# First loads, the order of hi and lo passes, and the issue of weight sums in a two-layer decoder trunk

## The chip, the cores and the metric

One Trainium2 chip, one core in use. The metric is the device time of one launch in microseconds (us). The time of the kernel before is the median of 3 runs; which of two kernels is the faster is judged from such runs.

## The reference

A two-layer trunk on x (256 tokens by 1024) with a memory of 256 rows by 1024, all in fp32. Cut to what matters here:

```python
# layer 0: short gated convolution; layer 1: block-sparse causal attention (one block of 256 here)
b_gate, c_gate, u = jnp.split(h @ w_in, 3, axis=-1)
x = x + (b_gate * causal_conv(c_gate * u)) @ w_out
# both layers: attention to the memory, 4 heads of 256
k, v = jnp.split(rms_norm(mem, g) @ w_kv, 2, axis=-1)
q = rms_norm(x, g) @ w_q
x = x + softmax(q k^T / 16) v @ w_o
# both layers: feed-forward, inner width 2816
g, u = jnp.split(rms_norm(x, g) @ w_gu, 2, axis=-1)
x = x + (silu(g) * u) @ w_down
# after layer 0 one shared k, v is projected from x for layer 1; a last rms_norm ends it
```

The weights are streamed from DRAM.

## The kernel before, in words

**Three passes for one product.** TensorE (PE) works on fp32 data in a rounded form (fp32r). To keep fp32 accuracy each operand is held as hi + lo: ScalarE (ACT) rounds a copy (hi), VectorE (DVE) subtracts it from the original (lo), and PE adds three products in PSUM: hi by hi and hi by lo with the weight's hi part, and lo by hi with the weight's lo part. The tables `(0, 0), (0, 1), (1, 0)` in the code are these passes, weight part first. A weight chunk's lo part is so needed by one pass of three.

**The weight stream.** `weight_plan` (line 69) lists all weight chunks in the order of their use; a chunk is 128x1024 fp32, 512 KB. `Feed` (line 314) moves each through SP's load queue into one of `RAWS` = 5 raw buffers, then through ACT (`split_high`) and DVE (`split_low`) into one of `WBUFS` = 10 pairs of hi and lo, and PE frees the pair. When the lo part of a chunk is made, its raw buffer is free, and the load five chunks on is written to SP's queue. The program is straight-line code for each engine, made at build time: `Clock` (line 184) keeps a rough model of the time of each engine, and `Side` (line 247) uses it to decide where splits, evictions, norms and attention steps go in each engine's order. An engine runs its instructions in that order; a wait at the head of a queue holds all that is behind it. `Feed.hooks` is a table of things to do when the load of a given number is issued.

**The order of the layers.** Keys of the memory for layer 0 (`mem_keys`, line 829, tiles `raw_memk`, `hi_memk`, `lo_memk`, `acc_memk`: eight chunks k, each times eight column groups j); the convolution (`short_conv`, chunks wc, wu, wb, PSUM tiles `cu` and `pb`, four pairs jp of two column groups jj); its output product; memory values and attention; the feed-forward of layer 0; the shared k, q and v of the block attention with keys, output and values of the memory beside them; memory attention; the feed-forward of layer 1; the last norm.

**The start.** `first` (128x568) holds a quarter of the memory, the first 256 columns of key chunk 0 and all gains in one tensor. The rest of chunk 0 comes in two loads (256 and 512 columns), then the second 256-column piece of the memory (`mT_raw`, 128x256), then chunk 1. While these come in, PE runs 13 products on a blank tile (`warm`).

**The feed-forward.** A norm needs a factor `rs` per token, which GpSimd (POOL) computes in one instruction for each of the two token halves h. While the factor of the second half is on its way, PE runs `rows` products (weights wr). `sg` is the silu on ACT, `gg` its product on DVE, `pt_g` the transpose of `gg` on PE. Gate and up weights are wg, wu, the down weights wd.

**Sums of weights.** Gate and up columns are worked on in 11 blocks of 256. For some pairs of blocks, named by their first block in `GROUPS` (8 in layer 0; 4 and 8 in layer 1), the weights of the pair are taken as four quarters B11, B12, B21, B22 and multiplied in a form with seven block products in place of eight (PSUM tile `seven`). It needs four sums, T1 = B11+B12, T3 = B12+B22, T2 = T1+B22, T4 = T2+B21, each in two halves. They are made in DRAM: `sum_steps` (line 532) gives 16 steps for a pair, eight copies on SP's queue (line 550, B to T or T to T) and eight adding transfers on POOL's queue (line 548, `accum_op`). A copy of a sum waits until the adding transfer before it has landed, and an adding transfer waits for its copy. In the kernel before, the steps hang at loads spread evenly: `SUMS_AT` puts layer 0's 16 steps over loads 44 to 104 and layer 1's 32 steps over loads 128 to 220 (lines 1031 to 1034). When their numbers come up, they are issued, whatever is in flight. The sums are read back as weight chunks (`raw_wT`).

**Bank of memory.** The hi and lo parts of the memory are put aside in DRAM and read back for layer 1 by two loads on POOL's queue (`mem_bank`, line 1627, row L1629 of the profile).

All ACT, DVE and POOL work that a helper records has line L242 in the profile, matmuls have L464, transposes L468, loads L481.

Of the kernel before, what the change touches and what calls it, by code (L numbers as in the profile page):

```python
# [42 lines left out]
SPARE = 1500  # L43
LATER = 2000
BANKWISE = 5
GROUPS = ((8,), (4, 8))
SUMS_AT = ((44, 104), (128, 220))

# [20 lines left out]
def weight_plan():  # L69
# [82 lines left out]
    plan = row_plan("memk0", mem_w_kv[0], 0, "memkv0", pieces=2, halves=2)  # L152
    plan[0].update(cuts=(0, T, 2 * T, D), pieces=4)
    for jp in range(4):
# [92 lines left out]
class Side:  # L247
# [3 lines left out]
    def __init__(self, clock, **free):  # L251
        self.clock = clock
        self.open = []
        self.free = {kind: [0.0] * n for kind, n in free.items()}
        self.feed = None

# [20 lines left out]
    def poll(self):  # L277
        for item in sorted(self.open, key=lambda i: i[0]):
            if not item[2] and item[0] <= self.clock.now:
                self.step(item)  # L280
        soon = any(self.clock.now <= i[0] <= self.clock.now + HOLD for i in self.open)
        self.feed.pump(soon)

    def others(self, item=None):
# [91 lines left out]


class Act:

# [19 lines left out]
def yoco_kernel(  # L399
    ctx: ExitStack,  # L400
    tc: tile.TileContext,
    x, mem, positions, norm_ffn, norm_final, xT, memT, first, chunks, conv_wT, out,
):
# [49 lines left out]
    def unit_f32(name, shape):  # L453
        return acts.tile(shape, F32, tag="unit", name=name)
# [32 lines left out]
    def load_chunk(it):  # L487
        raw = raws.tile([P, it["a"], it["b"]], F32, tag="raw", name=f"raw_{it['name']}")
        if "sum" in it:
            load(raw, weight_sums[it["sum"]])  # L490
            return raw
        src = chunks[it["chunk"] * P:(it["chunk"] + 1) * P].rearrange("p (a n) -> p a n", a=it["a"])
        for c in chunk_pieces(it)[1 if "cuts" in it else 0:]:
            load(raw[:, :, c], src[:, :, c], freed=feed.emptied)
        return raw
# [11 lines left out]
    def split_high(it, raw):  # L507
        hi = wts.tile([P, it["a"], it["b"]], F32R, tag="hi", name=f"hi_{it['name']}")
        lo = wts.tile([P, it["a"], it["b"]], F32R, tag="lo", name=f"lo_{it['name']}")
        for c in chunk_pieces(it):  # L510
            if it["gain"] is None:
                scalar.copy(hi[:, :, c], raw[:, :, c])
            elif "cuts" in it:
                scalar.activation(hi[:, 0, c], first_raw if c.start == 0 else raw[:, 0, c], AF.Copy, scale=first_gain)
            else:
                scalar.activation(hi[:, :, c], raw[:, :, c], AF.Copy, scale=gain_col(*it["gain"]))
        return hi, lo

    def split_low(it, raw, hi, lo):
        for c in chunk_pieces(it):  # L520
            if it["gain"] is None:
                vector.tensor_sub(lo[:, :, c], raw[:, :, c], hi[:, :, c])
            elif "cuts" in it:
                vector.scalar_tensor_tensor(lo[:, 0, c], first_raw if c.start == 0 else raw[:, 0, c], first_gain,
                                            hi[:, 0, c], op0=OP.mult, op1=OP.subtract)
# [32 lines left out]

    plan, _, quarters, ffn_steps = weight_plan()
    feed = side.feed = Feed(clock, plan, load_chunk, split_high, split_low)  # L560


# [188 lines left out]
    mT0 = new_act("mT0")  # L751
    first_tile = unit_f32("first", [P, 2 * T + len(GAINS) * KD])
    load(first_tile, first)
    first_mem, first_raw, first_gains = (first_tile[:, c] for c in (slice(0, T), slice(T, 2 * T), slice(2 * T, None)))
    first_gain = first_gains[:, :1]
# [5 lines left out]
    feed.load_to(1)  # L761
    m_turned = [half_tile("mT_raw_0", (P, 2, T))]
    load(m_turned[0][:, 1, :], memT[:P, T:])
    feed.load_to(2)
# [12 lines left out]
    feed.split_next()  # L777
    split(*m_parts[1], m_turned[0][:, 1, :])
    feed.split_next()
    split(*unit_pair(mT0, 1), m_turned[1])  # L780

    def split_rest():
        for i in (2, 3):
# [4 lines left out]
            vector.tensor_sub(lo, m_turned[i], hi)  # L788
        for _ in range(4):
            side.give("half")  # L790
# [38 lines left out]
    def mem_keys(name, mT, wait, scaled=True):  # L829
# [32 lines left out]
        for k in range(KD - 2):  # L862
            w = feed.take(f"{name}_{k}")
            if k == 0:
                for js in ((0, 1), (2, 3), (4, 5, 6, 7)):
                    for one in ((0, 0), (0, 1)):
                        for j in js:
                            step(k, w, j, (one,))
                for j in range(KD):
                    step(k, w, j, ((1, 0),))  # L870
                feed.free()
                continue
# [157 lines left out]
    for l in range(2):  # L1030
        steps = [step for jp in GROUPS[l] for step in sum_steps(l, jp)]
        first, end = SUMS_AT[l]
        for n, step in enumerate(steps):
            feed.hooks.setdefault(first + (end - first) * n // len(steps), []).append(step)


    def short_conv(act, into):
# [34 lines left out]
        for jp in range(4):  # L1072
# [7 lines left out]
            for jj in range(2):  # L1080
# [10 lines left out]
                for i, name in enumerate(("wc", "wu")):  # L1091
# [3 lines left out]
                    jobs.append(side.start(gate_sum(cus[0], pieces[0]) if i == 0 else conv(j, cus[1], pieces, jobs)))  # L1095
                mm_cols(pb, act, wb, jj, 1, last=0)
                mm_cols(pb, act, wb, jj, 0, range(1, KD), last=0)
                if jj:
# [609 lines left out]
def laid_out(inputs):  # L1708
# [16 lines left out]
    return dict(inputs, xT=pairs(inputs["x"][0]), memT=memT, first=first, chunks=chunks.reshape(-1, D),  # L1725
                conv_wT=columns(inputs["conv_w"][0]))


_INS = ["x", "mem", "positions", "norm_ffn", "norm_final", "xT", "memT", "first", "chunks", "conv_wT"]

# [17 lines left out]
```

## Time and profile before

| what | value |
|---|---|
| time, median of 3 runs (lowest to highest) | 786.16 us (785.79 to 787.91) |
| the profiled execution: its own time | 786.73 us |
| its span, first to last instruction | 785.0 us |
| PE busy, matmuls | 773.9 us (99%), 4147 |
| DVE busy | 573.5 us (73%), 872 |
| ACT busy | 459.5 us (59%), 728 |
| POOL busy | 37.7 us (5%), 68 |
| DRAM read and written | 178.82 MB and 28.31 MB |
| mean granted clock of PE | 0.999 |

The span is read on PE: the other engines run beside it. PE is idle for 785.0 - 773.9 = 11.1 us, at a few places, and a change that doesn't alter PE's work moves the time through these places or through new ones. A row of the timeline gives start, length, engine, line, operation, `out<-in`, the tile sizes, how many instructions run together, and in brackets how long the engine had been idle and on whom it had waited.

### The profile page before, as it was taken

Reading aid. Unit: us, or ns where it says so; the run is one execution under the profiler, and the core shown is the slowest. Engines: PE = TensorE matmul, PEld = TensorE weight load, DVE = VectorE, ACT = ScalarE, POOL = GpSimd, SP = SyncE. Lnnn points to the kernel's source line nnn. Section 1 sums busy time; section 2 is a strip of 40 time slices with the busy share of each in tenths; the row PEclk is TensorE's granted clock in tenths of the full one; section 3 lists DMA queues with packets and bytes.
Section 4 is the critical chain, followed back from the end, with each engine's and each line's share of the span. In section 5 each row is a group of like instructions: output and inputs, shape, how many; then the busy total and the mean of one; then the engine's idle time right before and its main releaser. Section 6 shows DMA issues by size and latency. Waiting matters only on the chain.

```text
span 785.0 us, 11228 instructions
## 1 busy us (share of the span) xinstructions
PE 773.9 (99%) x4147; PEld 664.1 (85%) x4147; DVE 573.5 (73%) x872; ACT 459.5 (59%) x728; POOL 37.7 (5%) x68
## 2 busy tenths in 40 slices
PE   8999999999999999999999999999999999999996
PEld 7988888898888888888888889888988788888885
DVE  5988888768786566687766557877868776966964
ACT  7875656665654555566564563655756456755741
POOL 1010001000100000000100010030001000000000
PEclk9999999999999999999999999999999999999999
DMA  9775988916676756699787456799746746956921
GB/s 336 282 270 192 280 298 226 371 66 214 191 256 226 230 166 209 211 364 315 232 296 253 181 162 231 279 276 322 201 146 189 261 152 219 323 168 213 339 116 53
DMA packets 48951, 182.71 MB, mean 233 GB/s; under 512 B 6272, under 2 KB 7552, under 8 KB 46720
## 3 DMA queue, kind: packets, MB, share of 16 engines
q1 hardware_dynamic: 46112, 166.79, 59.4%
q0 software_dynamic: 2208, 14.68, 9.2%
q8 instruction: 32, 0.52, 0.3%
q10 hardware_dynamic: 576, 0.52, 0.2%
q14 instruction: 23, 0.19, 0.1%
HBM read 178.82 MB, written 28.31 MB: 264 GB/s over the span
## 4 chain that ended last, share of the span: by engine, by line
PE 92%; DVE 3%; DMA 2%; issue 1%; ACT 1%; SPq 0%; POOLq 0%; DVEq 0%; ACTq 0%
PE gu L464 17%; PE ff L464 14%; PE seven L464 7%; PE q_acc L464 6%; PE acc_mo L464 6%; PE acc_memv L464 6%; PE cu L464 4%; PE acc_memk L464 4%; PE rows L464 4%; PE acc_v L464 3%; PE acc_q L464 3%; PE acc_o L464 3%; PE acc_cout L464 3%; PE acc_k L464 3%; PE pb L464 2%; PE po L464 2%
## 5 line engine op out<-in xcount | busy, mean ns | idle before, releaser
L464 PE MATMUL ff<-hi_wd,guT 128*128 128x512 f32 (+1 forms) x352 | 108.3, 388 | 0.0
L464 PEld LDWEIGHTS ff<-hi_wd,guT 128*128 128x128 f32 x352 | 65.8, 188 | 12.8
L464 PE MATMUL ff<-lo_wd,guT 128*128 128x512 f32 (+1 forms) x176 | 68.3, 388 | 0.0
L242 DVE TENSOR_TENSOR gu_sb<-gu_sb,gu 128x256 f32<-128x256 f32 x48 | 19.8, 421 | 59.0 <-ACT gu_sb L242 58.5
L242 DVE TENSOR_TENSOR lo_wd<-raw_wd,hi_wd 128x1024 fp32r<-128x1024 f32 x44 | 53.5, 1221 | 7.4 <-ACT hi_wd L242 7.4
L242 ACT CAST hi_wd<-raw_wd 128x1024 fp32r<-128x1024 f32 x44 | 46.1, 1051 | 15.6 <-DMA raw_wd<-in_chunks_dram 15.0
L242 ACT COPY gu_sb<-gu 128x256 f32<-128x256 f32 x48 | 17.7, 372 | 60.7 <-PE gu L464 60.7
L464 PE MATMUL gu<-ffn,hi_wg 128*128 128x512 f32 x192 | 48.0, 390 | 0.0
L464 PE MATMUL gu<-ffn,hi_wu 128*128 128x512 f32 x192 | 47.6, 390 | 0.0
L464 PE MATMUL acc_memk<-mT,hi_memk 128*128 128x256 f32 x256 | 46.2, 287 | 0.4 <-ACT hi_memk L242 0.4
L242 ACT CAST hi_wu<-raw_wu 128x1024 fp32r<-128x1024 f32 x32 | 33.5, 1050 | 15.4 <-DMA raw_wu<-in_chunks_dram 11.4
L464 PEld LDWEIGHTS gu<-ffn,hi_wg 128*128 128x128 f32 x192 | 35.9, 188 | 7.3
L464 PEld LDWEIGHTS gu<-ffn,hi_wu 128*128 128x128 f32 x192 | 35.8, 188 | 7.3
L464 PE MATMUL rows<-hi_wr,ffn 128*128 128x512 f32 x128 | 40.7, 395 | 0.0
L464 PE MATMUL acc_mo<-hi_mo,oT_mem 128*128 128x512 f32 x128 | 40.6, 393 | 0.0
L464 PEld LDWEIGHTS acc_memk<-mT,hi_memk 128*128 128x128 f32 x256 | 39.3, 193 | 1.2 <-ACT hi_memk L242 1.1
L242 DVE TENSOR_TENSOR lo_wu<-raw_wu,hi_wu 128x1024 fp32r<-128x1024 f32 x32 | 38.8, 1221 | 1.1 <-ACT hi_wu L242 1.0
L464 PE MATMUL acc_memv<-hi_memv,mT 128*128 128x512 f32 x128 | 39.5, 390 | 0.0
L464 PEld LDWEIGHTS ff<-lo_wd,guT 128*128 128x128 f32 x176 | 33.2, 188 | 6.3
L242 POOL TENSOR_TENSOR rs<-ms,neg_half 128x1 f32<-128x1 f32 x14 | 13.5, 964 | 471.0 <-DVE ms L242 461.8
L464 PE MATMUL acc_memk<-mT,lo_memk 128*128 128x256 f32 x128 | 34.7, 288 | 0.8 <-DVE lo_memk L242 0.8
L464 PE MATMUL q_acc<-mem,hi_mq 128*128 128x512 f32 x128 | 32.4, 394 | 0.0
(276 smaller groups left out, 1955.3 us busy)
## 6 DMA issues: line engine op xcount, KB each, us to landing
raw_wd<-in_chunks_dram SPq DMA_DIRECT2D x44, 512.0 KB, 5.2
raw_wu<-in_chunks_dram SPq DMA_DIRECT2D x32, 512.0 KB, 4.8
T<-in_chunks_dram POOLq DMA_DIRECT2D x24, 512.0 KB, 7.9
raw_wg<-in_chunks_dram SPq DMA_DIRECT2D x24, 512.0 KB, 5.3
raw_wT<-T SPq DMA_DIRECT2D x24, 512.0 KB, 4.7
raw_wB<-in_chunks_dram SPq DMA_DIRECT2D x18, 512.0 KB, 5.0
raw_memv<-in_chunks_dram SPq DMA_DIRECT2D x16, 512.0 KB, 5.1
raw_mq<-in_chunks_dram SPq DMA_DIRECT2D x16, 512.0 KB, 7.2
```

Source lines behind the costliest of these rows:

```text
L242: return call(out, *args, **kw)
L464: nc.tensor.matmul(o, l, r, start=start, stop=stop)
```

## The change

Four things are changed.

1. **First loads in three issues.** Key chunk 0 is cut at 256, 768 and 1024 columns (before at 256, 512 and 1024). A new input `second` holds columns 256 to 768 of the chunk in its first 128 rows, and in its next 128 rows the last 256 columns of the chunk beside the memory piece that had its own load. So `first`, the two halves of `second` and chunk 1 follow each other in SP's queue; one issue less stands ahead of chunk 1. PE takes the column groups of chunk 0 in the order (0, 1), (2 to 5), (6, 7).

2. **Lo parts later in the first keys.** For chunks 1, 2 and 3 of layer 0's keys PE runs the 16 products with the hi part for all eight column groups first and the eight with the lo part after them. Before, each group had its two hi products and its lo product together, so that the lo part was wanted with the third product.

3. **Lo parts later in the convolution.** `pb` takes the products with hi_wb first and those with lo_wb at the end.

4. **Sums one by one.** A class `Sums` holds the steps. A step is issued when five raw buffers are loaded and not yet split, the model's transfer time is over, and 4,000 ns of the model (`APART`) have gone since the step before; or at the latest by the load number of an even spread over the windows in `SUMS_AT`, which are now one for each pair: loads 44 to 104, 104 to 200 and 200 to 250.

The core of the diff:

```diff
-SUMS_AT = ((44, 104), (128, 220))
+SUMS_AT = (((44, 104),), ((104, 200), (200, 250)))
...
-    plan[0].update(cuts=(0, T, 2 * T, D), pieces=4)
+    plan[0].update(cuts=(0, T, 3 * T, D))
...
         self.feed.pump(soon)
+        self.sums.pump()
...
+class Sums:
+    def add(self, steps, first, end):
+        for n, step in enumerate(steps):
+            at = first + (end - first) * n // len(steps)
+            self.steps.append((first, at, step))
+            self.feed.hooks.setdefault(at, []).append(lambda at=at: self.until(at))
+
+    def until(self, at):
+        while self.steps and self.steps[0][1] <= at:
+            self.next()
+
+    def next(self):
+        self.steps.pop(0)[2]()
+        self.after = self.clock.now + APART
+
+    def pump(self):
+        if not self.steps or self.steps[0][0] > self.feed.loaded or self.clock.now < self.after:
+            return
+        if self.feed.loaded - self.feed.lows >= RAWS and self.clock.free["dma"] <= self.clock.now:
+            self.next()
...
+        if "cuts" in it:
+            load(raw[:, 0, T:3 * T], second[:P])
+            return raw
...
-    m_turned = [half_tile("mT_raw_0", (P, 2, T))]
-    load(m_turned[0][:, 1, :], memT[:P, T:])
+    load(first_tile[:, gained:], second[P:])
...
-                for js in ((0, 1), (2, 3), (4, 5, 6, 7)):
+                for js in ((0, 1), (2, 3, 4, 5), (6, 7)):
...
+            if not scaled and k < 4:
+                for ones in (((0, 0), (0, 1)), ((1, 0),)):
+                    for j in range(KD):
+                        step(k, w, j, ones)
+                feed.free()
+                continue
...
-                mm_cols(pb, act, wb, jj, 1, last=0)
-                mm_cols(pb, act, wb, jj, 0, range(1, KD), last=0)
+                mm_cols(pb, act, wb, jj, 0, range(1, KD))
+                mm_cols(pb, act, wb, jj, 1)
```

Line numbers of the changed kernel differ: its loads are L513, its matmuls L496, its sum steps L583 (POOL) and L585 (SP), its ACT, DVE and POOL work L243.

SP at the program's start, before (`in_chunks_dram` is the weight stream, `in_memT_dram` the memory):

```order
L481 DMA first<-in_first_dram 128x568
L481 DMA raw_memk_0_117<-in_chunks_dram 128x256
L481 DMA raw_memk_0_117<-in_chunks_dram 128x512
L481 DMA mT_raw_120<-in_memT_dram 128x256
L481 DMA raw_memk_1_122<-in_chunks_dram 128x512 x2
```

and now:

```order
L513 DMA first<-in_first_dram 128x568
L513 DMA raw_memk_0_117<-in_second_dram 128x512
L513 DMA first<-in_second_dram 128x512
L513 DMA raw_memk_1_120<-in_chunks_dram 128x512 x2
L513 DMA mT_raw_123<-in_memT_dram 128x512
```

Chunk 1 moved from the fifth issue to the fourth.

PE at the end of the first column group of the convolution (jp 0, jj 0; hi_wb_1 is the second chunk of wb), before:

```order
L464 MATMUL cu<-mix_1_275,lo_wu_1_543 128x256 x4
L464 MATMUL pb<-mix_0_274,lo_wb_0_558 128x256 x4
L464 MATMUL pb<-mix_1_275,lo_wb_1_570 128x256 x4
L464 MATMUL pb<-mix_0_274,hi_wb_0_557 128x512 x3
L464 MATMUL pb<-mix_1_275,hi_wb_1_569 128x512 x4
```

and now:

```order
L496 MATMUL cu<-mix_1_279,lo_wu_1_541 128x256 x4
L496 MATMUL pb<-mix_0_278,hi_wb_0_555 128x512 x3
L496 MATMUL pb<-mix_1_279,hi_wb_1_567 128x512 x4
L496 MATMUL pb<-mix_0_278,lo_wb_0_556 128x256 x4
L496 MATMUL pb<-mix_1_279,lo_wb_1_568 128x256 x4
```

The seven products with hi_wb moved ahead of the eight with lo_wb.

POOL from the norm ahead of layer 1's memory attention to that ahead of its feed-forward (`T_1_8` is layer 1's pair 8, the digit behind it the half; T1, T2, T3 and T4 of half 0 have the numbers 513, 515, 517 and 519 before and 511, 513, 515 and 517 now; each norm has two `rs`, one for each half of the tokens), before:

```order
L242 TENSOR_TENSOR rs<-ms,neg_half 128x1
L548 DMA T_1_8_0_513<-in_chunks_dram 64x2048
L548 DMA T_1_8_1_514<-in_chunks_dram 64x2048
L242 TENSOR_TENSOR rs<-ms,neg_half 128x1
L548 DMA T_1_8_0_517<-in_chunks_dram 64x2048
L548 DMA T_1_8_1_518<-in_chunks_dram 64x2048
L548 DMA T_1_8_0_515<-in_chunks_dram 64x2048
L548 DMA T_1_8_1_516<-in_chunks_dram 64x2048
L242 TENSOR_TENSOR rs<-ms,neg_half 128x1 x2
L548 DMA T_1_8_0_519<-in_chunks_dram 64x2048
L548 DMA T_1_8_1_520<-in_chunks_dram 64x2048
```

and now:

```order
L583 DMA T_1_4_1_510<-in_chunks_dram 64x2048
L1671 DMA mT_1_4725<-mem_aside_494 128x2048
L243 TENSOR_TENSOR rs<-ms,neg_half 128x1 x2
L583 DMA T_1_8_0_511<-in_chunks_dram 64x2048
L243 TENSOR_TENSOR rs<-ms,neg_half 128x1
L583 DMA T_1_8_1_512<-in_chunks_dram 64x2048
L583 DMA T_1_8_0_515<-in_chunks_dram 64x2048
L243 TENSOR_TENSOR rs<-ms,neg_half 128x1
L583 DMA T_1_8_1_516<-in_chunks_dram 64x2048
L583 DMA T_1_8_0_513<-in_chunks_dram 64x2048
L583 DMA T_1_8_1_514<-in_chunks_dram 64x2048
```

Behind the last `rs` of the feed-forward's norm there stood the two adding transfers of T4; now one of T3 stands there, with one of T1 and one of T3 between the two `rs`, and those of T2 and T4 come later. The load of the memory's second part (`mT_1`) now stands behind all of pair 4's transfers; before it stood ahead of those of T4.

More of the change, by code (lines that the diff above doesn't have):

```diff
@@ L44 @@
 LATER = 2000
+APART = 4000
 BANKWISE = 5
 GROUPS = ((8,), (4, 8))
-SUMS_AT = ((44, 104), (128, 220))
+SUMS_AT = (((44, 104),), ((104, 200), (200, 250)))
 class Rows:
@@ L254, in __init__ @@
         self.free = {kind: [0.0] * n for kind, n in free.items()}
-        self.feed = None
+        self.feed = self.sums = None
     def start(self, gen):
@@ L375, in free, with __init__ @@
         self.freed += n
+class Sums:
+    def __init__(self, clock, feed):
+        self.clock, self.feed = clock, feed
+        self.steps = []
+        self.after = 0.0
+    def add(self, steps, first, end):
[14 more added lines that the diff above has]
+            self.next()
 class Act:
@@ L401, in yoco_kernel @@
     tc: tile.TileContext,
-    x, mem, positions, norm_ffn, norm_final, xT, memT, first, chunks, conv_wT, out,
+    x, mem, positions, norm_ffn, norm_final, xT, memT, first, second, chunks, conv_wT, out,
 ):
@@ L492, in load_chunk @@
         src = chunks[it["chunk"] * P:(it["chunk"] + 1) * P].rearrange("p (a n) -> p a n", a=it["a"])
-        for c in chunk_pieces(it)[1 if "cuts" in it else 0:]:
+        if "cuts" in it:
+            load(raw[:, 0, T:3 * T], second[:P])
+            return raw
+        for c in chunk_pieces(it):
             load(raw[:, :, c], src[:, :, c], freed=feed.emptied)
@@ L513, in split_high @@
             elif "cuts" in it:
-                scalar.activation(hi[:, 0, c], first_raw if c.start == 0 else raw[:, 0, c], AF.Copy, scale=first_gain)
+                scalar.activation(hi[:, 0, c], {0: first_raw, 3 * T: last_raw}.get(c.start, raw[:, 0, c]), AF.Copy, scale=first_gain)
             else:
@@ L523, in split_low @@
             elif "cuts" in it:
-                vector.scalar_tensor_tensor(lo[:, 0, c], first_raw if c.start == 0 else raw[:, 0, c], first_gain,
+                vector.scalar_tensor_tensor(lo[:, 0, c], {0: first_raw, 3 * T: last_raw}.get(c.start, raw[:, 0, c]), first_gain,
                                             hi[:, 0, c], op0=OP.mult, op1=OP.subtract)
@@ L560, in yoco_kernel @@
     feed = side.feed = Feed(clock, plan, load_chunk, split_high, split_low)
+    sums = side.sums = Sums(clock, feed)
     def mm_rows(acc, act, k, h, w, b, start, stop):
@@ L751, in yoco_kernel @@
     mT0 = new_act("mT0")
-    first_tile = unit_f32("first", [P, 2 * T + len(GAINS) * KD])
-    load(first_tile, first)
-    first_mem, first_raw, first_gains = (first_tile[:, c] for c in (slice(0, T), slice(T, 2 * T), slice(2 * T, None)))
+    gained = 2 * T + len(GAINS) * KD
+    first_tile = unit_f32("first", [P, gained + 2 * T])
+    load(first_tile[:, :gained], first)
+    last_raw, second_mem = first_tile[:, gained:gained + T], first_tile[:, gained + T:]
+    first_mem, first_raw, first_gains = (first_tile[:, c] for c in (slice(0, T), slice(T, 2 * T), slice(2 * T, gained)))
     first_gain = first_gains[:, :1]
@@ L761, in yoco_kernel @@
     feed.load_to(1)
-    m_turned = [half_tile("mT_raw_0", (P, 2, T))]
-    load(m_turned[0][:, 1, :], memT[:P, T:])
+    load(first_tile[:, gained:], second[P:])
+    m_turned = [None]
     feed.load_to(2)
@@ L777, in yoco_kernel @@
     feed.split_next()
-    split(*m_parts[1], m_turned[0][:, 1, :])
+    split(*m_parts[1], second_mem)
     feed.split_next()
@@ L788, in split_rest @@
             vector.tensor_sub(lo, m_turned[i], hi)
-        for _ in range(4):
+        for _ in range(3):
             side.give("half")
@@ L1030, in yoco_kernel @@
     for l in range(2):
[L1031 to L1034, printed above, removed]
+        for jp, window in zip(GROUPS[l], SUMS_AT[l]):
+            sums.add(sum_steps(l, jp), *window)
     def short_conv(act, into):
@@ L1724, in laid_out @@
     first = np.concatenate([memT[:P, :T], chunks[0][:, :T], columns(*norms)], axis=1)
-    return dict(inputs, xT=pairs(inputs["x"][0]), memT=memT, first=first, chunks=chunks.reshape(-1, D),
+    second = np.concatenate([chunks[0][:, T:3 * T], np.concatenate([chunks[0][:, 3 * T:], memT[:P, T:]], axis=1)])
+    return dict(inputs, xT=pairs(inputs["x"][0]), memT=memT, first=first, second=second, chunks=chunks.reshape(-1, D),
                 conv_wT=columns(inputs["conv_w"][0]))
-_INS = ["x", "mem", "positions", "norm_ffn", "norm_final", "xT", "memT", "first", "chunks", "conv_wT"]
+_INS = ["x", "mem", "positions", "norm_ffn", "norm_final", "xT", "memT", "first", "second", "chunks", "conv_wT"]
 def kernel(**inputs):
```

## The prediction

> **What bounds the kernel now.** I read the head of the page first, then PE's waits, then busy time by stretches, and last the timeline around each wait.
>
> ```profile
> span 785.0 us, 11228 instructions
> PE 773.9 (99%) x4147; PEld 664.1 (85%) x4147; DVE 573.5 (73%) x872; ACT 459.5 (59%) x728; POOL 37.7 (5%) x68
> ```
>
> PE is the bound: it does matmuls in 773.9 of 785.0 us, and the change takes none of them away. All that can be won is PE's idle time, 11.1 us. The view of waits lists what released PE (sum in us, times, longest):
>
> ```profile
> PE pt_g L468 <- DVE gg L242: 1.6, 1, 1.6
> PE warm L464 <- DVE blank L758: 1.5, 1, 1.5
> PE acc_memk L464 <- DVE lo_memk L242: 0.8, 2, 0.5
> PE pb L464 <- DVE lo_wb L242: 0.5, 2, 0.3
> PE acc_memk L464 <- ACT hi_memk L242: 0.4, 1, 0.4
> ```
>
> Stretches of the span (length, PE busy, PEld, DVE, ACT, POOL, granted clock, share of the DMA engines, GB/s):
>
> ```profile
> 5.00:10.00 5.00, 4.36 (x33) 3.77 (x32) 3.14 (x6) 3.12 (x5) 0.00 (x0) 1.00 0.99 369
> 10.00:15.00 5.00, 4.48 (x38) 4.28 (x37) 3.95 (x5) 4.45 (x8) 0.00 (x0) 1.00 1.04 412
> 25.00:30.00 5.00, 5.00 (x43) 4.93 (x42) 5.00 (x9) 5.00 (x10) 0.00 (x0) 1.00 0.64 238
> 700.00:785.00 85.00, 78.73 (x398) 66.62 (x396) 58.81 (x87) 42.57 (x63) 1.46 (x2) 0.99 0.49 174
> ```
>
> The last 85 us hold 85.00 - 78.73 = 6.3 us of the idle time, which the change doesn't touch; nor does it touch the 1.5 us before `warm`. What is left is 3.3 us in three places: the first keys (0.8 + 0.4), the convolution's `pb` (0.5), and one transpose `pt_g` in layer 1's feed-forward (1.6). Each of the change's parts aims at one of them.
>
> **The first keys.** Rows of PE, then of ACT, DVE and SP at the start:
>
> ```profile
> 4.25 1.48 PE L464 MATMUL acc_memk<-mT,hi_memk 128*128 128x256 f32 x8
> 6.09 1.22 PE L464 MATMUL acc_memk<-mT,hi_memk 128*128 128x256 f32 x8 [0.36 <-ACT hi_memk L242]
> 9.04 0.39 PE L464 MATMUL acc_memk<-mT,lo_memk 128*128 128x256 f32 x1 [0.28 <-DVE lo_memk L242]
> 9.50 0.28 PE L464 MATMUL acc_memk<-mT,lo_memk 128*128 128x256 f32 x1
> 12.70 0.39 PE L464 MATMUL acc_memk<-mT,lo_memk 128*128 128x256 f32 x1 [0.52 <-DVE lo_memk L242]
> 25.48 0.39 PE L464 MATMUL acc_memk<-mT,lo_memk 128*128 128x256 f32 x1
> 22.44 1.15 ACT L242 ACTIVATE hi_memk<-raw_memk,g_cols 128x1024 fp32r<-128x1024 f32 x1 [0.32 <-DMA raw_memk<-in_chunks_dram]
> 24.15 1.28 DVE L242 SCALAR_TENSOR_TENSOR lo_memk<-raw_memk,g_cols,hi_memk 128x1024 fp32r<-128x1024 f32 x1
> 1.18 0.89 SPq L481 DMA_DIRECT2D raw_memk<-in_chunks_dram  x2
> 2.11 0.43 SPq L481 DMA_DIRECT2D mT_raw<-in_memT_dram  x1
> 2.59 0.91 SPq L481 DMA_DIRECT2D raw_memk<-in_chunks_dram  x2
> ```
>
> At 9.04 and 12.70 PE waits 0.28 and 0.52 us for the lo part of chunks 1 and 2. A matmul behind a wait takes 0.39 instead of 0.28, so each wait costs another 0.11: 0.80 + 0.22 = 1.02 us. With 16 hi products ahead, the lo part is wanted 14 matmuls later, and PE's step is about 0.12 us (worked out below): 1.6 us, more than either wait. I count both as gone. The 0.36 at 6.09 I count at nothing won: PE now has four products ready instead of eight before it needs the piece of 512 columns, so the wait comes earlier (four of the 1.48 us end near 5.0), but that piece is issued first at 1.18 and not second. Bounds for this item: if its hi part is ready at 6.09 again, twelve products stand behind it instead of eight, 4 x 0.13 ((1.22 - 0.28)/7) = 0.5 us lost; if it comes before 5.0, 0.47 won (0.36 + 0.11).
>
> One issue less stands ahead of chunk 1: it is issued at 2.11 instead of 2.59, 0.48 us earlier. It can land that much earlier, or not at all where the DMA engines are the limit: their share is 0.99 and then 1.04 from 5 to 15 us. I take 0.3 for the supply, between 0 and 0.48. The Trainium skill, page "DMA: Bandwidth & Descriptors", section "Issuing engines are not separate DMA queues", says that initiation costs sequencer time, usually small beside the transfer itself; by that the value is 0, and the sum below would be 0.2 us smaller.
>
> What is late next is chunk 7. Its lo part is ready at 24.15 + 1.28 = 25.43, and PE takes it at 25.48: 0.05 us to spare. PE earlier than that must wait, unless the lo part also comes earlier. DVE works back to back there behind an add that hangs on PE itself (a broadcast of the norm's factor), and ACT waits for chunk 7's load until 22.44, so hi is ready at 23.59. So DVE can come forward by at most 24.15 - 23.59 = 0.56 without an earlier load, and by 0.86 with 0.3 us of it. Of 1.02 won, I keep **0.8**; bounds: 0.05 (all given back at chunk 7) and 1.9 (1.02 + 0.47 + all of the 0.48).
>
> **The convolution.** Rows of PE at the first column group, with the matching wait of the second pair:
>
> ```profile
> 35.21 1.12 PE L464 MATMUL cu<-mix,lo_wu 128*128 128x256 f32 x8
> 36.17 0.64 PE L464 MATMUL pb<-mix,lo_wb 128*128 128x256 f32 x4
> 37.10 0.74 PE L464 MATMUL pb<-mix,lo_wb 128*128 128x256 f32 x4 [0.30 <-DVE lo_wb L242]
> 37.68 1.76 PE L464 MATMUL pb<-mix,hi_wb 128*128 128x512 f32 x7
> 54.41 0.74 PE L464 MATMUL pb<-mix,lo_wb 128*128 128x256 f32 x4 [0.17 <-DVE lo_wb L242]
> ```
>
> Eight lo products step from 35.21 to 36.17, 0.12 us each, so four from 36.17 end their steps at 36.65 and the next starts at 37.10: 0.45 lost where the wait column says 0.30, and 0.10 more for the first matmul behind it (0.74 against 0.64). The second place, by the same difference of 0.15, loses 0.17 + 0.15 + 0.10 = 0.42. Together 0.97. The seven hi products, some 1.6 us, now stand before the lo ones and cover both waits, even with PE 0.8 earlier. What is late next is DVE: it is busy in all of 25 to 30 us, so a PE that comes earlier finds its other splits nearer. I take **0.8** of 0.97; bounds 0.0 and 0.97. Nothing else waits for the order of passes inside `pb`; its eviction comes behind the last of them either way.
>
> **The sums of weights.** The chain around the wait of `pt_g`, and its twin in layer 0, where PE doesn't wait:
>
> ```profile
> 599.64 1.62 POOL L548 DMA_DIRECT2D T<-in_chunks_dram  x2
> 604.46 1.47 SPq L481 DMA_DIRECT2D raw_wd<-in_chunks_dram  x2
> 613.43 0.39 PE L464 MATMUL rows<-hi_wr,ffn 128*128 128x512 f32 x1
> 613.57 1.05 ACT L242 CAST hi_wd<-raw_wd 128x1024 fp32r<-128x1024 f32 x1 [0.20 <-DMA raw_wd<-in_chunks_dram]
> 614.52 0.38 ACT L242 ACTIVATE sg<-rows 128x256 f32<-128x256 f32 x1
> 615.41 0.44 PE L468 MATMUL pt_g<-ident,gg 128*128 128x128 f32 x2 [1.59 <-DVE gg L242]
> 211.64 0.41 SPq L481 DMA_DIRECT2D raw_wd<-in_chunks_dram  x1
> 218.03 1.05 ACT L242 CAST hi_wd<-raw_wd 128x1024 fp32r<-128x1024 f32 x1 [1.05 <-DMA raw_wd<-in_chunks_dram]
> raw_wd<-in_chunks_dram SPq DMA_DIRECT2D x44, 512.0 KB, 5.2
> T<-in_chunks_dram POOLq DMA_DIRECT2D x24, 512.0 KB, 7.9
> ```
>
> PE waits for `gg`, `gg` for `sg`, and `sg` stands on ACT behind the split of a down weight whose load came late: issued by SP around 605.5 (the second of the pair from 604.46), landed by 613.57, some 8 us. In front of it two adding transfers were issued from 599.64; at a median of 7.9 us each they were still moving. In layer 0 the second such load, issued at 211.64, took until 218.03, 6.4 us, and the median is 5.2.
>
> The change puts three adding transfers around these norms, but only one behind the second `rs`, at about 599.7; the other two follow the first `rs`, about 6 us earlier, and by the median have landed when the loads start. From the start of the split to `pt_g` it is 615.41 - 613.57 = 1.84. With 6.4 us the split starts at 611.9, `pt_g` could run at 613.74, and PE is there at 613.43 + 0.23 (the step of `pb`'s x7: (1.76 - 0.39)/6) = 613.66: 0.1 lost. With 5.2 nothing is lost. Start to start the wait costs 615.41 - 613.66 = 1.75. I take **1.5**, bounds 0 and 1.75.
>
> Elsewhere the new places of 48 steps may make waits that are not there now. All waits that the view lists lie at the places above, so each new one has to use up a reserve first; I put down **0.2** lost, bounds 0 and 2.
>
> **The sum.** 0.8 + 0.8 + 1.5 - 0.2 = 2.9 us. The profiled execution took 786.73 (its span of 785.0 and 1.7 around it), so one like it would take 783.8; the median is 0.57 below that execution, which gives 783.3 for the median. The bounds together: 1.9 + 0.97 + 1.75 = 4.6 won, 781.5; and 0.05 - 2 = 2 lost, 788.1.
>
> **The rivals.**
>
> *The early gain is given back (A).* Chunk 7's 0.05 us and DVE's full 5.00 from 25 to 30 speak for it; the slow start of the stream against it. The keys give 0.05, `pb` 0.5, `pt_g` 1.5, less 0.2: 1.85 won, 784.3, within what counts as no change (0.3% of 786.16 is 2.4 us, about what a measurement of this kernel can tell).
>
> *The late load stays late (B).* One adding transfer is still in flight at 604.46, and the two before it can have a backlog: three take 3 x 512 KB of reads and as many writes. If the load again needs 8 us, the 1.5 is gone: 1.4 won, 784.8. For it: 8 us beside two of them, where the median load takes 5.2. Against it: only one is young. The same page, section "Queues, rings and completion order", states that each DMA engine takes turns between its queues packet by packet. By that a load beside an adding transfer gets a share of each engine in any case, which speaks for B; the 8 us against 5.2 agree with sharing.
>
> *A wait behind the longer chain on POOL (C, slower).* The second part of the memory is read back by POOL, now behind all of pair 4's transfers:
>
> ```profile
> L1629 POOL DMA_DIRECT2D mT<-mem_aside x2: 553/569/585, 412.1 to 455.2; - x2
> L464 PE MATMUL acc_memk<-mT,hi_memk x128: 278/283/467, 463.7 to 492.2; 128*128 128x256 f32 x128
> DMA to landing us min/median/max: 5.8/7.8/9.8
> ```
>
> It is issued at 455.2 and first wanted halfway through these keys, near 478. With up to 9.8 us to land it must be issued by 468. Ahead of it POOL now adds T2, waits for SP's copies to T4 and adds T4. In the emitted order the last of these stands by PE products that run near 462 now, so I place the issue at 462 to 464. Each us beyond 468 is one lost. At 474 it is 6 lost, and 6 - 3.1 = 2.9 slower: 789.1. It decides from a delay of about 11 us against the place I give it.
>
> *Nothing comes of it (D).* The loads land as before, DVE stays the limit, new waits eat the rest: 786.2, within 0.5.
>
> **Chances.** The forecast 0.55; A 0.15, B 0.14, C 0.06, D 0.10. The forecast's own spread (782 to 784.3) is mostly below 783.8: 0.48 of its 0.55 is faster by over 0.3%, and of A and B 0.09. So faster 0.57, slower 0.07 (C, and 0.01 of D), no change the rest, 0.36. The range runs from 781.4, the bound of all gains, to 786.2, which takes in A, B and half of D.
>
> **What would show it.** Right: no row with `lo_memk` or `lo_wb` among PE's waits, `pt_g` without a wait or under 0.3 us, `raw_wd` in layer 1 landing within 6.5 us, and PE's first `pb` product of the convolution 0.5 to 1.2 us earlier than before. Wrong: a new wait on `lo_memk` at chunk 4 or 7 near 25 us (A), a `pt_g` wait over 1 us (B), a wait on `mT` near 478 (C), or any new row of over 0.5 us between 60 and 560 us, above all behind a sum.

## The result, and the profile after

The changed kernel takes 795.27 us (median of 7 runs, 790.27 to 796.68) against 786.16 (median of 7, 784.85 to 787.91): ratio 1.0105, 95% interval 1.0076 to 1.0133. It is slower by some 8 to 9 us, where 2.9 less had been forecast, and it lies outside the range. Its runs also spread over 6.4 us, those of before over 3.1.

The head of its page:

```profile
span 794.8 us, 11233 instructions
PE 777.5 (98%) x4147; PEld 666.2 (84%) x4147; DVE 573.5 (72%) x872; ACT 458.5 (58%) x728; POOL 37.0 (5%) x68
```

PE's idle time is now 794.8 - 777.5 = 17.3 us, 6.2 more than before. PE's busy time has grown as well, by 3.6 us, although it runs the same 4147 matmuls. Both together are the 9.8 us by which the span grew. The view of PE's waits, to be held against that of before:

```profile
PE pt_g L500 <- DVE gg L243: 2.2, 1, 2.2
PE pt_g L500 <- DVE p L243: 1.6, 1, 1.6
PE q_acc L496 <- DVE memv L243: 1.5, 2, 1.1
PE warm L496 <- DVE blank L796: 1.5, 1, 1.5
PE pt_r L500 <- DVE r L243: 1.2, 1, 1.2
PE gu L496 <- DVE gu_sb L243: 1.0, 1, 1.0
PE s L496 <- ACT q L243: 0.9, 1, 0.9
PE acc_memk L496 <- DVE lo_memk L243: 0.6, 1, 0.6
PE acc_memk L496 <- ACT hi_memk L243: 0.3, 1, 0.3
```

The rows of `pb` are gone, and so is the transpose near 613 us: the `pt_g <- gg` here is its twin of layer 0, near 224 us, where nothing waited before. Five places wait that did not: the memory's queries of layer 0 (`q_acc`, `s`, 148 to 155 us), that twin (224), a gate and up product (`gu`, 309), the rotary step (`pt_r`, 421) and a transpose of layer 1 (`pt_g <- p`, 696).

The stretches that hold them (length, PE busy, PEld, DVE, ACT, POOL, granted clock, DMA share, GB/s) show where the idle time lies:

```profile
140.00:180.00 40.00, 37.44 (x218) 32.74 (x218) 26.52 (x51) 25.27 (x46) 0.00 (x0) 0.96 0.54 196
180.00:226.00 46.00, 43.78 (x223) 36.48 (x221) 34.32 (x49) 25.27 (x39) 4.43 (x5) 1.00 0.77 236
226.00:260.00 34.00, 34.00 (x168) 28.98 (x169) 26.60 (x40) 17.98 (x31) 0.79 (x1) 0.95 0.63 202
560.00:620.00 60.00, 60.00 (x339) 51.92 (x338) 43.11 (x72) 36.89 (x68) 5.21 (x6) 1.00 0.66 189
620.00:700.00 80.00, 78.43 (x382) 65.58 (x381) 60.03 (x77) 45.01 (x64) 3.12 (x4) 1.00 0.80 273
```

From 560 to 620 us, the stretch that the change had to mend, PE is full. The loss is elsewhere. The granted clock falls below 1 behind the first two places, which is where the longer busy time comes from.

**The costliest place: 148 to 155 us.** POOL's rows there:

```profile
126.47 0.55 POOL L243 TENSOR_TENSOR rs<-ms,neg_half 128x1 f32<-128x1 f32 x1 [9.24 <-DVE turns L243]
126.97 2.59 POOL L583 DMA_DIRECT2D T<-in_chunks_dram  x3
130.63 0.78 POOL L583 DMA_DIRECT2D T<-in_chunks_dram  x1 [1.08 <-DMA T<-in_chunks_dram]
```

and the same rows before:

```profile
127.65 0.55 POOL L242 TENSOR_TENSOR rs<-ms,neg_half 128x1 f32<-128x1 f32 x1 [9.25 <-DVE turns L242]
128.15 2.58 POOL L548 DMA_DIRECT2D T<-in_chunks_dram  x3
143.93 0.78 POOL L548 DMA_DIRECT2D T<-in_chunks_dram  x1 [13.20 <-DMA T<-in_chunks_dram]
```

Four adding transfers, given "one by one", are issued within 3.7 us of each other. Three came in a burst before as well, since they all stand behind the `rs`, which waits for DVE. The fourth waited for its copy until 143.93; now SP's order has that copy earlier (issued at 125.08, before at 132.99), and it joins the burst. The chain of waits shows what that does to the weight load that PE needs next:

```profile
131.42 14.41 DMA raw_mq<-in_chunks_dram
145.93 1.06 ACT hi_mq L243
```

14.4 us from issue to landing. Before, the loads issued from 130 to 138 us took 7.7 to 9.8.

**The other places** are no bursts: one or two adding transfers are in flight beside a load that PE hangs on soon. At 224: one at 215.08, just as the second `raw_wd` goes out at 215.57 (the two of 202.42 and a copy of 209.69 had landed). At 309: two, at 296.08 and 299.90, beside a load at 300.64 that takes 7.2. At 421: one at 409.67 and the memory's 1 MB at 410.25, beside a load at 411.26 that takes 7.4. At 696: two, at 680.09 and 685.45, beside a load at 684.47 that takes 9.7.

```profile
215.57 8.47 DMA raw_wd<-in_chunks_dram
684.47 9.72 DMA raw_wd<-in_chunks_dram
```

**Where the model's times went.** The class `Sums` keeps 4 us between two steps by the build-time clock. For layer 0's first four adding transfers that clock says 133.9, 140.7, 155.5 and 159.5 us; they were issued at 127.0, 127.6, 128.2 and 130.6. For pair 8 of layer 1 it puts the second to fourth at 559.0, 563.1 and 568.5; they ran at 602.6, 603.2 and 609.7. Not all of these last 40 us is waiting behind an `rs`: the clock itself lags by then, since the first of the pair, which it puts at 546.8, goes out at 574.3 when it is held to its place in the program (an experiment below). POOL's queue knows nothing of that clock: an instruction runs when the one before it is done and its own inputs are there. Behind the copies it runs ahead, behind an `rs` it is held and then lets go of a burst.

**What a load pays.** From each trace I took every weight load of 512 KB from 30 us on, counted the adding transfers in flight 1 us after its issue, and took the median time to landing:

| adding transfers in flight | 0 | 1 | 2 | 3 | 4 |
|---|---|---|---|---|---|
| before: us (loads) | 4.8 (213) | 6.6 (36) | 8.2 (13) | 9.5 (3) | none |
| after: us (loads) | 4.7 (225) | 6.9 (29) | 9.7 (7) | 11.6 (2) | 14.3 (2) |

Each one more in flight goes with 1.3 to 2.8 us more. After the change fewer loads meet an adding transfer at all, 40 against 52. The rule of one by one did thin them out; it is the few tight meetings that cost.

### The profile page after: what moved, and what is told of

Its sections match the earlier page's. It is cut to its first block, busy times and chain, and to the rows that moved or that the text cites. A ratio compares the mean times of both kernels' runs of the same rounds, so it can differ in the third digit from the quotient of the medians.

```text
span 794.8 us, 11233 instructions
## 1 busy us (share of the span) xinstructions
PE 777.5 (98%) x4147; PEld 666.2 (84%) x4147; DVE 573.5 (72%) x872; ACT 458.5 (58%) x728; POOL 37.0 (5%) x68
## 4 chain that ended last, share of the span: by engine, by line
PE 87%; DMA 5%; DVE 3%; ACT 1%; issue 1%; POOLq 0%; DVEq 0%; ACTq 0%; SPq 0%
PE gu L496 16%; PE ff L496 14%; PE seven L496 7%; PE cu L496 6%; PE acc_mo L496 6%; PE q_acc L496 5%; PE rows L496 4%; PE acc_memk L496 4%; PE acc_memv L496 3%; PE pb L496 3%; PE acc_v L496 3%; PE acc_o L496 3%; PE acc_cout L496 3%; PE acc_k L496 3%; PE acc_q L496 3%; DMA raw_wd<-in_chunks_dram 2%
## 5 line engine op out<-in xcount | busy, mean ns | idle before, releaser
L496 PE MATMUL ff<-hi_wd,guT 128*128 128x512 f32 (+1 forms) x352 | 107.7, 387 | 0.0
L496 PEld LDWEIGHTS ff<-hi_wd,guT 128*128 128x128 f32 x352 | 65.8, 188 | 12.8
L496 PE MATMUL ff<-lo_wd,guT 128*128 128x512 f32 (+1 forms) x176 | 68.3, 388 | 0.0
L243 DVE TENSOR_TENSOR gu_sb<-gu_sb,gu 128x256 f32<-128x256 f32 x48 | 19.8, 420 | 55.8 <-ACT gu_sb L243 55.5
L243 ACT CAST hi_wd<-raw_wd 128x1024 fp32r<-128x1024 f32 x44 | 46.1, 1050 | 14.5 <-DMA raw_wd<-in_chunks_dram 13.5
L243 DVE TENSOR_TENSOR lo_wd<-raw_wd,hi_wd 128x1024 fp32r<-128x1024 f32 x44 | 53.2, 1219 | 1.7 <-ACT hi_wd L243 1.5
L243 ACT COPY gu_sb<-gu 128x256 f32<-128x256 f32 x48 | 17.8, 373 | 59.2 <-PE gu L496 59.1
L496 PE MATMUL gu<-ffn,hi_wg 128*128 128x512 f32 x192 | 48.1, 391 | 1.0 <-DVE gu_sb L243 1.0
L496 PE MATMUL gu<-ffn,hi_wu 128*128 128x512 f32 x192 | 47.5, 390 | 0.0
L243 ACT CAST hi_wu<-raw_wu 128x1024 fp32r<-128x1024 f32 x32 | 33.5, 1052 | 20.2 <-DMA raw_wu<-in_chunks_dram 14.4
L496 PE MATMUL acc_memk<-mT,hi_memk 128*128 128x256 f32 x256 | 43.6, 285 | 0.4 <-ACT hi_memk L243 0.3
L496 PEld LDWEIGHTS gu<-ffn,hi_wg 128*128 128x128 f32 x192 | 35.8, 188 | 8.6 <-DVE gu_sb L243 1.4
L496 PE MATMUL rows<-hi_wr,ffn 128*128 128x512 f32 x128 | 41.9, 404 | 0.0
L496 PEld LDWEIGHTS gu<-ffn,hi_wu 128*128 128x128 f32 x192 | 35.8, 188 | 7.3
L496 PE MATMUL acc_mo<-hi_mo,oT_mem 128*128 128x512 f32 x128 | 40.5, 393 | 0.0
L243 DVE TENSOR_TENSOR lo_wu<-raw_wu,hi_wu 128x1024 fp32r<-128x1024 f32 x32 | 38.8, 1219 | 1.8 <-ACT hi_wu L243 1.8
L496 PE MATMUL acc_memv<-hi_memv,mT 128*128 128x512 f32 x128 | 39.7, 391 | 0.0
L496 PEld LDWEIGHTS acc_memk<-mT,hi_memk 128*128 128x128 f32 x256 | 37.6, 191 | 1.3 <-ACT hi_memk L243 1.1
L496 PEld LDWEIGHTS ff<-lo_wd,guT 128*128 128x128 f32 x176 | 33.1, 188 | 6.3
L243 POOL TENSOR_TENSOR rs<-ms,neg_half 128x1 f32<-128x1 f32 x14 | 13.6, 970 | 455.2 <-DVE ms L243 445.9
L496 PE MATMUL q_acc<-mem,hi_mq 128*128 128x512 f32 x128 | 32.9, 398 | 1.5 <-DVE memv L243 1.5
L243 DVE TENSOR_TENSOR lo_wg<-raw_wg,hi_wg 128x1024 fp32r<-128x1024 f32 x24 | 28.8, 1219 | 5.0 <-ACT hi_wg L243 4.9
```

Of the source, the lines that this page charges most:

```text
L243: return call(out, *args, **kw)
L496: nc.tensor.matmul(o, l, r, start=start, stop=stop)
```

## The experiments

Theory: the weight loads that PE hangs on next are late because adding transfers are in flight beside them, at the first place in a burst, and they are there by POOL's own order, not by the plan. Rivals: the early parts move PE ahead of its supply; the changed order on ACT and DVE makes the waits; the places of the sums are wrong however they are issued. Each group shared one chip, and each median stands against the median of the kernel before on it.

### Parts apart (the kernel before: 785.67 us)

**Even spread of the sums, with the new loads and passes.**

```diff
-SUMS_AT = (((44, 104),), ((104, 200), (200, 250)))
+SUMS_AT = (((44, 104),), ((128, 174), (174, 220)))
-        self.sums.pump()
```

> The changed kernel with the sums' 16 + 32 steps back at loads spread evenly over 44 to 104 and 128 to 220; first loads and pass orders as changed. Theory (the new places of the sums cost the time): the gain of the early parts is left, 1.5 to 2.5 us below the kernel before, 783.7 to 784.7, with the one pt_g wait of 1.6 to 1.8 us near 612 back. Rival (the early parts move PE ahead of its supply and make the later waits): 789 to 795, with waits near 148, 223, 308, 420 and 694 us.

784.57 us, ratio 0.9985 (0.9976 to 0.9994). The later waits are gone, so the early parts are not their cause. The `pt_g` near 612 did not wait in this execution, against both expectations: PE's waits are only these.

```profile
PE warm L495 <- DVE blank L795: 1.5, 1, 1.5
PE acc_memk L495 <- DVE lo_memk L243: 0.5, 1, 0.5
```

**The new sums alone**: the kernel before with the class `Sums` and its windows.

> The kernel before with the new issue of the sums alone. Theory (the sums cost the time): 792 to 799, with waits of over 1 us on the memory's queries near 150 us, on a pt_g near 224 and another near 695. Rival (early parts are the cause): within 2 us of the kernel before, 784 to 788.

794.46 us, ratio 1.0130 (1.0097 to 1.0162). The new issue of the sums is enough by itself. The places are the same; `gu` near 310 waits longer.

```profile
PE gu L496 <- DVE gu_sb L243: 2.4, 1, 2.4
PE pt_g L500 <- DVE gg L243: 2.2, 1, 2.2
PE pt_g L500 <- DVE p L243: 1.7, 1, 1.7
```

**No adding transfers.**

```diff
                 if add:
-                    nc.gpsimd.dma_start(dst, src, accum_op=OP.add, max_dma_last_dim=8192)
+                    pass
```

> The changed kernel without the 24 adding transfers on POOL's queue, so that each T holds a copy of one quarter and not a sum; all else in its place, the order on PE, ACT and DVE too. Theory (adding transfers stand in the way of the weight loads): none of the later waits is over 0.5 us, 781 to 784. Rival (the new order on ACT and DVE makes the waits, not the transfers): the five places still wait, 790 to 796. Rival (the copies on SP's queue are to blame): 787 to 792, with the waits that follow a copy left (near 224 and 308).

783.55 us, ratio 0.9974 (0.9965 to 0.9984). With the order on PE, ACT and DVE and the copies on SP as in the changed kernel, all five places are free.

```profile
PE warm L496 <- DVE blank L796: 1.5, 1, 1.5
PE acc_memk L496 <- DVE lo_memk L243: 0.2, 1, 0.2
```

A copy that followed an adding transfer waits for none here. So neither the order on those engines nor the copies alone make the waits.

**The two pass orders alone**, on the kernel before (the second and third part of the diff).

> The kernel before with the two pass orders alone (hi before lo in key chunks 1 to 3 and in pb). Theory: pb's two waits are gone and with them 0.9 us; the keys win 0.5 to 0.9 and give part of it back at chunk 7; 784.4 to 785.3. Rival (the early gain is all given back at chunk 7 or by DVE): 785.8 to 786.5.

785.59 us, ratio 0.9994 (0.9985 to 1.0003): within the noise, between 1.2 won and 0.2 lost, and between the two expectations. The `pb` waits are gone; at chunk 7 of the keys a wait of 0.60 us has come, as the first rival of the prediction has it, and one on the hi part of chunk 0 was 0.92 in this execution.

### Which transfer, and held or not (the kernel before: 786.36 us)

**Five of 24 left out**, one for each place.

```diff
-                if add:
+                if add and (l, jp, name, i) in OUT:
+                    pass
+                elif add:
+OUT = ((0, 8, "T3", 1), (0, 8, "T4", 0), (1, 4, "T1", 1), (1, 4, "T2", 0), (1, 8, "T4", 1))
```

> The changed kernel without five of its 24 adding transfers, one for each place that waits: the last of layer 0's four near 131 us, layer 0's first T4 near 215, pair 4's second T1 near 300, pair 4's first T2 near 410, and pair 8's second T4 of layer 1 near 685; the five sums so lack a part. Theory (a load is late by some 2.4 us for each adding transfer in flight, and one too many is enough): the waits near 148, 223 and 308 us fall under 0.6 us, those near 420 and 694 at least by half; 783.5 to 786.5. Rival (the load on DMA over long stretches, not the single neighbour): each wait keeps three quarters of its size, 790 to 793.

784.60 us, ratio 0.9974 (0.9963 to 0.9986).

```profile
PE s L497 <- ACT q L244: 0.9, 1, 0.9
PE q_acc L497 <- DVE memv L244: 0.7, 1, 0.7
```

Four places are free with one transfer less each, and the ratio is the same as with all 24 left out. The first place keeps 1.6 of its 2.4 us (the expectation was under 0.6). Three adding transfers are in flight there as in the kernel before, and the copy still comes early. The three took 9.4, 12.0 and 14.6 us to land, where those of the kernel before took 5.3, 7.5 and 10.2, and the three loads issued from 128 to 131 us took 12.8 to 13.2, against 12.0 to 14.4 with the fourth transfer and 9.5 to 9.8 before (issued from 130 to 133). So most of the lateness at the costliest place seems to come with the copy's earlier issue and the lesser part with the fourth transfer; no run moves the copy alone. By itself it does no harm: without adding transfers beside it the same loads took 4.4 to 5.3.

**Layer 0 even, layer 1 one by one.**

```diff
-        self.sums.pump()
+        if self.feed.loaded > 104:
+            self.sums.pump()
```

> The changed kernel with layer 0's 16 steps at evenly spread loads as before, layer 1's one by one as changed. Theory (each place has its own cause): the waits near 148 and 223 us and the half-rate stretches behind them go, some 5 and 4 us; those near 308, 420 and 694 stay, 1 to 2.5 each; 785.5 to 788.5. Rival (the late loads push each other on, and the first collision makes the rest): all five go, 783 to 785.

789.20 us, ratio 1.0034 (1.0022 to 1.0046), somewhat over the expectation. The two places of layer 0 are free, the three of layer 1's sums stay: each has its own cause, and layer 0's are the larger part of the loss.

```profile
PE pt_g L501 <- DVE p L243: 2.0, 1, 2.0
PE pt_r L501 <- DVE r L243: 1.6, 1, 1.6
PE gu L497 <- DVE gu_sb L243: 1.3, 1, 1.3
```

**Even, with pair 8's last two ahead of the `rs`.**

```diff
-SUMS_AT = (((44, 104),), ((104, 200), (200, 250)))
+SUMS_AT = (((44, 104),), ((128, 174), (174, 212)))
-        self.sums.pump()
```

> The changed kernel's loads and passes, the sums evenly spread as before, with layer 1's pair 8 over loads 174 to 212 and not 220, so that its last two adding transfers stand ahead of the two rs of layer 1's feed-forward and not behind them. Theory (a load that PE's next step hangs on must have none in flight): no pt_g wait near 612 in any execution, 783.0 to 784.4, at or below the kernel with the even spread alone. Rival (the two meet other loads on their new place): 785 to 787 with a wait between 560 and 590 us.

784.68 us, ratio 0.9976 (0.9965 to 0.9986), beside 0.9985 for the plain even spread: the intervals overlap. No `pt_g` wait in the profiled execution, but one on `acc_mo` near 577 us, where the transfers now stand:

```profile
PE acc_mo L495 <- DVE oT_mem L243: 0.9, 1, 0.9
```

Both expectations hold in part. Moving the two shows no sign of the 1.5 us that the prediction gave it.

**POOL held to the program's place.** Ahead of each adding transfer POOL reads one column of the lo part that DVE made last in the order, so the transfer goes out no sooner than that.

```diff
+        self.last_lo = self.ready[n][1][:, 0, :1].bitcast(F32)
...
+                    nc.gpsimd.tensor_tensor(anchor, feed.last_lo, neg_half, op=OP.mult)
                     nc.gpsimd.dma_start(dst, src, accum_op=OP.add, max_dma_last_dim=8192)
```

> The changed kernel with one small POOL instruction ahead of each adding transfer, which reads the last lo part that stands ahead of it in DVE's order; POOL so can't issue the transfer before the program's own place is reached. Theory (POOL runs ahead of the model's times and issues in bursts): the four of layer 0 no longer meet the query loads, the wait near 148 us goes, the one near 223 falls; 784 to 790. Rival (the places themselves are wrong, held or not): 792 to 797.

783.51 us, ratio 0.9959 (0.9945 to 0.9972). One small instruction ahead of each transfer, same plan, same order, all transfers: the loss is turned into a gain, and this is below both kernels. No wait is left behind 30 us.

### The held version again, and three controls (the kernel before: 786.17 us)

**The same kernel once more.**

> The anchored kernel once more, for a narrower interval. Theory: 783.2 to 784.2, ratio to the kernel before 0.995 to 0.998. Rival (the first result was a lucky draw of few runs): 785 to 787.

783.02 us (782.79 to 783.48), ratio 0.9962 (0.9950 to 0.9975). Its runs spread over 0.7 us, those of the kernel before over 3. POOL at the first place:

```profile
141.67 0.19 POOL L584 TENSOR_TENSOR anchor<-lo_mq,neg_half 128x1 f32<-128x1 f32 x1 [14.31 <-DVE lo_mq L243]
141.92 0.96 POOL L585 DMA_DIRECT2D T<-in_chunks_dram  x1
147.91 0.18 POOL L584 TENSOR_TENSOR anchor<-lo_mo,neg_half 128x1 f32<-128x1 f32 x1 [5.03 <-DVE lo_mo L243]
148.34 0.79 POOL L585 DMA_DIRECT2D T<-in_chunks_dram  x1 [0.25 <-issue]
```

The reading instruction waits 14.31 us for its lo part, and the first transfer goes out at 141.92 instead of 127. In the whole trace no load meets more than two adding transfers (43 meet one, 4 two).

**Held, but evenly spread.**

> The changed kernel's loads and passes, sums evenly spread as before, with the anchors. Theory (what counts is that POOL keeps to the program's places; even or one by one matters little): 783.2 to 784.8, no wait over 0.6 us behind 60 us save perhaps the pt_g near 612, where two transfers still stand behind the last rs. Rival (one by one is worth something by itself): 784.6 to 786, at or above the even spread without anchors.

785.06 us, ratio 0.9992 (0.9981 to 1.0002). Here the rival comes out: held and even is not better than even alone. 68 loads meet an adding transfer, against 47 in the held one-by-one kernel, and PE waits 1.1 us on `pt` near 440. So holding is not enough by itself; the plan counts too. This kernel also has the older windows, loads 128 to 174 and 174 to 220, so whether it is the rule of one by one or its wider windows that counts is not shown: the wider windows, held and evenly spread, were not run.

**First loads alone**, on the kernel before (the first part of the diff).

> The kernel before with the first loads in three issues alone. Theory (one issue less, chunk 1 earlier by 0.4 us; the lo waits of the keys and of pb stay): 0.2 to 1.0 us below the kernel before, 785.2 to 786.2. Rival (the loads are all of the early gain): 1.0 to 1.8 below.

785.22 us, ratio 0.9991 (0.9982 to 1.0000): 0.7 us, about half of the early gain, with an interval that reaches down to nothing. Against the expectation the lo waits of the keys are gone with the loads alone. In this execution `pt_g` near 613 waited 1.0 us and the first `pb` 0.3.

**New windows, even spread, not held.**

```diff
-        self.sums.pump()
```

> The changed kernel without the rule of one by one: its new windows, evenly spread, no anchors. In its order three adding transfers of layer 1's pair 8 stand right behind the last rs of layer 1's feed-forward and are ready when it is done. Theory (2.4 us of lateness for each in flight): no wait near 148 and 223 us, pt_g near 612 waits 2.5 to 6 us and a half-rate stretch follows; 787 to 792. Rival (the rule of one by one is what harms, windows don't): 783.5 to 785.5.

794.31 us, ratio 1.0107 (1.0092 to 1.0122), over the upper end of the expectation.

```profile
PE pt_g L499 <- DVE gg L243: 3.7, 1, 3.7
PE ff L495 <- DVE lo_wd L243: 2.0, 1, 2.0
```

POOL behind the last `rs` of layer 1's feed-forward:

```profile
596.61 1.39 POOL L243 TENSOR_TENSOR rs<-ms,neg_half 128x1 f32<-128x1 f32 x1 [5.74 <-DVE ms L243]
597.95 3.25 POOL L582 DMA_DIRECT2D T<-in_chunks_dram  x4
```

Four at once where three had been expected, at a place named ahead from the order alone. They take 8.3, 10.6, 13.4 and 16.0 us to land, and since they are issued 0.5 us apart they land some 3 us apart; the down weight issued at 602.78 takes 10.2. So a plan without the rule of one by one can lose as much when its transfers pile up behind an `rs`. The rule is not cleared by this: layer 0's window is 44 to 104 in every version, and there the rule without holding made the two waits that the even spread doesn't have.

## Why the prediction was wrong, point by point

- **The step that failed** is "Elsewhere the new places of 48 steps may make waits that are not there now ... I put down 0.2 lost, bounds 0 and 2." Against the even spread with the same early parts the new issue costs 1.0105 / 0.9985 = 1.2%, some 9.4 us. The 0.2 has no row behind it: I had not worked out when each of the 48 steps would run and which load would be in flight beside it. Where I did place one, the memory's second part, I went by the PE products that it stands beside in the emitted order, and so took an order for a time. On POOL that doesn't hold for the sums. Held to their places (an experiment above), the transfers of 215.08, 299.90 and 409.67 go out at 226.73, 356.89 and 415.87, so they had run ahead of the program by 6 to 57 us, and in layer 0 POOL's queue held a row of four that was free to run once the `rs` was done. The trace of before showed such a row already, three within 1.3 us behind the `rs` at 127.65. I read these rows for one place only, near 600 us. The sign that I had named last, new waits of over 0.5 us between 60 and 560 us, is what came.
- **What hid the cost from the sum**: I counted waits and not reserves. That PE waited nowhere between 60 and 560 us was taken for safety; a reserve of a few us, as the loads beside three transfers at 128 us had it, was used up by one transfer and one copy more.
- **The sums' own place.** "Only one behind the second `rs`" held: 602.55 for two and 609.69 for one, and `pt_g` near 613 no longer waits. The size was wrong: the 1.5 was that of one execution. In the even spread with the early parts the wait was absent, in the loads alone 1.0. The kernel with the two transfers moved and nothing else differs from the even spread by 0.1% (0.9976 and 0.9985), and the intervals overlap.
- **The first keys**, 0.8. The 9.04 and 12.70 waits went. Chunk 7 then waited, 0.56 us in the changed kernel and up to 1.1 in the held one, as the rival of the early gain said. The 1.02 was read too low: from one column group's first product to the next is 0.36 us undisturbed (9.26 to 9.62) and 1.01 and 1.14 at the two waits (8.25 to 9.26, 11.78 to 12.92), which is 1.43 lost. Yet PE reached the convolution only 0.44 earlier (29.94 against 30.38), and in the other traces with all the early parts between 29.12 and 30.86, so one trace can't size this term. The first loads alone measured 0.7 us (interval 0 to 1.4), which can't be put down to the one issue less, since they also cut chunk 0 in other places. The Trainium skill, page "DMA: Bandwidth & Descriptors", section "Issuing engines are not separate DMA queues", calls initiation time usually small beside the transfer itself; by that the value is nothing, and the interval doesn't exclude it.
- **`pb`**, 0.8: both waits went, and PE's own time from the first `cu` product to the memory's queries fell by 0.7 (by 0.3 against the loads alone, where one wait of 0.3 was left). Right. Keys and `pb` together measured 1.2 us (0.5 to 1.9) in the even spread, 1.6 forecast.
- **The rivals.** "The early gain is given back" was right in kind at chunk 7, not in full. "The late load stays late" named the mechanism, a share of the engines for each adding transfer, but looked for it only where the change was aimed; the table by number in flight is what it would have needed. The Trainium skill, page "DMA: Bandwidth & Descriptors", section "Queues, rings and completion order", has the engines take turns between queues; the 14.4 us beside four against 4.7 beside none agree with such sharing. The landings some 3 us apart look as if the adding transfers mostly queue behind each other. The slower rival, the memory's second part read too late, did not come: it was issued at 465.18, and PE did not wait for it.
- **The chance of slower**, 0.07, was tied to that one mechanism. The same kind of collision at places that I had not looked at should have had more. That the held kernel comes to 783.0 to 783.5, the time forecast for the change, doesn't bear out the sum: the early parts measured 1.2 us, and the rest of its gain was not taken apart.

## What to carry to other kernels

A plan made with a build-time clock held on POOL's queue only when something on the queue tied the instruction to its place in the program. For transfers that run on a free queue, read from the trace when they really go, what holds them, and what is released together behind each hold; a small instruction that reads something the program makes at the wished place is enough of a tie. Ask of every moved transfer which load will be in flight beside it and how late that load may be; here leaving out five of the 24 transfers won back as much as leaving out all of them.

## What the runs showed of the hardware

**Idle PE and its clock.** Behind waits of a certain length PE ran at half rate. The changed kernel's twin:

```profile
223.13 0.39 PE L496 MATMUL rows<-lo_wr,ffn 128*128 128x512 f32 x1
223.36 0.39 PE L496 MATMUL rows<-hi_wr,ffn 128*128 128x512 f32 x1
225.96 0.63 PE L500 MATMUL pt_g<-ident,gg 128*128 128x128 f32 x2 [2.21 <-DVE gg L243]
226.24 0.78 PE L496 MATMUL rows<-hi_wr,ffn 128*128 128x512 f32 x1
226.81 0.63 PE L496 MATMUL rows<-lo_wr,ffn 128*128 128x512 f32 x1
227.24 1.05 PE L496 MATMUL rows<-hi_wr,ffn 128*128 128x512 f32 x2
228.09 0.63 PE L496 MATMUL rows<-lo_wr,ffn 128*128 128x512 f32 x1
228.52 1.05 PE L496 MATMUL rows<-hi_wr,ffn 128*128 128x512 f32 x2
229.37 0.46 PE L496 MATMUL rows<-lo_wr,ffn 128*128 128x512 f32 x1
229.67 0.62 PE L496 MATMUL rows<-hi_wr,ffn 128*128 128x512 f32 x2
```

Steps are 0.43 us where they were 0.22 to 0.23 before the wait, for some 3 us. The clock in such stretches:

```profile
156.00:158.00 2.00, 2.00 (x9) 1.82 (x9) 1.24 (x3) 0.20 (x1) 0.00 (x0) 0.55 0.79 305
226.00:229.00 3.00, 3.00 (x9) 2.43 (x10) 1.88 (x3) 0.76 (x2) 0.00 (x0) 0.51 0.83 306
```

A wait of 2.2 us costs another 1.5 so, seven steps longer by 0.21. Over all runs the single waits of 1.6 and 1.7 us had no such stretch behind them (before, at 615; the new sums alone, at 700), one of 1.98 had none (layer 0 even, at 688) and one of 1.97 had one (new windows, at 697), those of 2.2, 2.4 and 3.7 had one. Three waits of 0.5, 1.1 and 0.9 us within 6 us, at 148 to 154, had one too; two of 0.7 and 0.9 there (five left out) had none. The Trainium skill, page "TensorE: Matmul & The Clock Gate", section "Part 1: The HAM clock gate (the "warmup" mystery)", tells of a gate at half or full rate that falls back behind an idle window of about 3.4 us; half and full agree with these rows, while here 1.97 us of idle time were enough once. So the waits cost more than their length: of the 9.8 us by which the span grew, 3.6 are busy time.

**Spread.** The runs of the changed kernel spread over 6.4 us and those of the held one over 0.7 and 1.0, but the held even spread and the kernel without five transfers, with few waits, have 4.1 each, so no rule follows.
